# Where VectorE's program begins in its instruction memory: place 8 in place of place 72 behind a boundary of 128

## The chip, the cores and the metric

The kernel runs on one core of one Trainium2 chip. The metric is the time of one execution on the device, in microseconds (us). Three executions of the kernel before took 162.50, 162.59 and 162.71 us; their median is 162.59 us.

## What is computed

The reference rotates pairs of numbers (a rotary embedding) in a tensor of 16 x 512 x 1024 numbers of 32 bits, seen as 16 heads of 64 numbers each:

```python
x = x.reshape(batch, seq, num_heads, head_dim)        # 16, 512, 16, 64
x1, x2 = x[..., :32], x[..., 32:]
cos, sin = cos[None, :, None, :], sin[None, :, None, :]   # 512 x 32, shared by batch and head
rotated = np.concatenate([x1 * cos - x2 * sin, x1 * sin + x2 * cos], axis=-1)
```

So 33.6 MB come in, 33.6 MB go out, and each output needs two products and a sum. The two tables are 64 KB each.

## The kernel before

The input is cut into eight tiles of 4 MB (`NT = 8`): 128 partitions, each with eight rows of 1024 numbers. There are five buffers for a whole tile (`bufs`, name `x_sb`), and the result overwrites the input in place. Tile 0 is loaded in pieces of 1, 1, 2 and 4 rows, tile 1 in two pieces, the others whole. Tiles 5 to 7 go into the buffers of tiles 0 to 2, so their loads wait for the stores of these.

All loads of x and all stores are issued by SyncE's queue (SP) in one fixed order: loads 0 to 4, stores 0 to 2, loads 5 to 7, stores 3 to 7 (L178 to L188; the last store in three pieces, rows 0 to 2, 6 to 7, then 3 to 5). The two tables are loaded from ScalarE's queue (L90, L91). Every one of these transfers is cut into equal parts, one per DMA engine, of which there are 16, and it is complete when all 16 have ended their part. So each of the 16 moves the same number of bytes of x over the whole run.

The tables are spread to 128 partitions by four small matmuls (L113), and ScalarE writes the signed sine table (L118, L119). Each tile is then computed in groups of two or three rows, in an order written out by hand (`PLAN`): T multiplies the rows, halves swapped, by the signed sine table on GpSimd (L146; B is the same on VectorE), P multiplies them by the cosine on VectorE (L149), S adds the two on VectorE (L151). For some groups A does the product in place on VectorE (L153) and M adds with TensorE and ScalarE instead (L158 to L161).

Before all of that, L69 places VectorE's program. `addr_align(128, offset, max_nops=0)` asks the loader to put the next instruction of VectorE's stream `offset` places behind a multiple of 128 instruction places. The places in between are padding; with `max_nops=0` VectorE does not execute the padding but jumps over it. Nothing else of the program depends on that number.

In the trace VectorE has 82 instructions. Two belong to the opening barrier, then comes the jump of L69 (at 0.76 us, 47 ns). Behind it stand 79: the 48 tensor operations, 27 waits on semaphores that are instructions of their own, and four of the closing barrier. With the first of them in place 72, the 57th is in place 128: it is the wait ahead of the sum (L151) that starts at 112.10 us. The last is in place 150.

Of the kernel before, what the change touches and what calls it, by code (L numbers as in the profile page):

```python
# [12 lines left out]
def kernel(  # L13
# [8 lines left out]
    nc = tc.nc  # L22
# [43 lines left out]

    SYNC = mybir.DependencyInfo(mybir.DependencyClass.Sync, mybir.DependencyReason.DATA)

    nc.vector.addr_align(128, 72, max_nops=0)  # L69

    def implied(inst, *others):
        for o in others:
# [151 lines left out]
```

## Time and profile before

| what | value |
|---|---|
| median of three executions | 162.59 us |
| the profiled execution's own time | 162.54 us |
| its span, first to last instruction | 160.8 us |
| VectorE (DVE) busy | 138.4 us, 86% |
| GpSimd (POOL) busy | 130.2 us, 81% |
| TensorE (PE) busy | 61.1 us, 38% |
| ScalarE (ACT) busy | 14.1 us, 9% |
| DMA: bytes moved, mean rate | 67.25 MB, 418 GB/s |

The profile is of one execution. Its span is 1.74 us shorter than its own time; the rest lies ahead of the first and behind the last instruction. In the profile L149 is line 149 of the kernel. DVE is VectorE, POOL is GpSimd, SP is SyncE, and SPq or DVEq is the queue of that engine (waits, barriers and the issue of transfers). A DMA queue's row gives its packets, its megabytes and the time that these took as a share of all 16 DMA engines over the stretch asked for. The queue of kind "instruction" is the one that brings pieces of program.

### The profile page before, as it was taken

To read this page: it belongs to the slowest core of one execution; us is meant where nothing else is said; L and a number is where in the kernel's file an instruction comes from. 1 tells how busy PE (TensorE), PEld (TensorE's weight loads), DVE (VectorE), ACT (ScalarE), POOL (GpSimd) and SP (SyncE) were. 2 spreads that over 40 slices of the span, in tenths; PEclk is the share of its full clock that TensorE was granted. 3 is DMA by queue.
4 is the path that set the end of the run, shared out by engine and by line. 5 is a ranking of instruction groups with operands and counts; after the bars stand their busy time and mean duration, and the time that the engine had idled before them with its cause. 6 is when DMAs were issued, how large, how long until landed. Compare 5 with 4: busy or idle time off the path is not lost.

```text
span 160.8 us, 395 instructions
## 1 busy us (share of the span) xinstructions
PE 61.1 (38%) x84; PEld 18.8 (12%) x84; DVE 138.4 (86%) x48; ACT 14.1 (9%) x25; POOL 130.2 (81%) x29
## 2 busy tenths in 40 slices
PE   0500000140488803088881368877686800000000
PEld 0200000100122100032221022222222200000000
DVE  0069999999999999999999999999999999999200
ACT  3110000000011110011110011111212110000000
POOL 2299999999979299995999299999999999991000
PEclk9999999999999995555558555599999985555555
DMA  5999999999999999999999999999999999999994
GB/s 157 388 438 421 452 461 457 391 432 465 408 400 465 440 391 465 448 391 465 448 391 457 457 391 440 457 410 424 440 432 424 432 448 416 432 457 400 407 432 205
DMA packets 3329, 67.25 MB, mean 418 GB/s; under 512 B 384, under 2 KB 512, under 8 KB 768
## 3 DMA queue, kind: packets, MB, share of 16 engines
q1 hardware_dynamic: 3168, 67.11, 97.8%
q10 hardware_dynamic: 160, 0.13, 0.3%
q14 instruction: 1, 0.01, 0.0%
HBM read 33.69 MB, written 33.55 MB: 418 GB/s over the span
## 4 chain that ended last, share of the span: by engine, by line
DVE 81%; issue 5%; POOL 3%; DMA 3%; PE 1%; ACT 0%; DVEq 0%
DVE x_sb L151 38%; DVE pp L149 36%; DVE x_sb L153 6%; POOL T L146 3%; DMA tabs<-in_sin_dram 3%; DVE T L146 1%; PE pp L113 1%; ACT sns L118 0%; DVEq L151 0%; ACT sns L119 0%; DVEq L149 0%
## 5 line engine op out<-in xcount | busy, mean ns | idle before, releaser
L146 POOL TENSOR_TENSOR T<-x_sb,sns 128x3072 f32<-128x3072 f32 (+1 forms) x22 | 129.2, 5914 | 14.4 <-ACT sns L119 5.4
L149 DVE TENSOR_TENSOR pp<-x_sb,tab 128x3072 f32<-128x3072 f32 (+1 forms) x20 | 60.8, 3040 | 9.3 <-ACT tab L119 8.8
L151 DVE TENSOR_TENSOR x_sb<-T,pp 128x3072 f32<-128x3072 f32 (+1 forms) x20 | 60.7, 3033 | 2.0 <-POOL T L146 0.5
L158 PE MATMUL ps<-T,ident 128*128 128x512 f32 x40 | 31.8, 886 | 42.6 <-POOL T L146 27.2
L160 PE MATMUL ps<-x_sb,ident 128*128 128x512 f32 x40 | 29.9, 839 | 18.9 <-DVE x_sb L153 18.9
L161 ACT COPY x_sb<-ps 128x512 f32<-128x512 f32 x20 | 11.7, 586 | 108.7 <-PE ps L160 108.7
L158 PEld LDWEIGHTS ps<-T,ident 128*128 128x128 f32 x40 | 7.8, 245 | 66.4 <-ACT x_sb L161 29.2
L160 PEld LDWEIGHTS ps<-x_sb,ident 128*128 128x128 f32 x40 | 9.9, 259 | 36.0 <-DVE x_sb L153 24.4
L153 DVE TENSOR_TENSOR x_sb<-x_sb,tab 128x2048 f32<-128x2048 f32 x5 | 11.4, 2280 | 0.0
L146 DVE TENSOR_TENSOR T<-x_sb,tab 128x2048 f32<-128x2048 f32 x3 | 6.8, 2281 | 0.0
L113 PE MATMUL pp<-tabs,sel 64*128 64x256 f32 x2 | 1.2, 694 | 5.1 <-DMA tabs<-in_sin_dram 5.1
L113 PE MATMUL tab<-tabs,sel 64*128 64x256 f32 x2 | 1.2, 710 | 0.8 <-DMA tabs<-in_cos_dram 0.8
L118 ACT ACT_TABLE_LOAD x1 | 1.3, 1283 | 1.9 <-issue 1.9
L113 PEld LDWEIGHTS pp<-tabs,sel 64*128 64x128 f32 x2 | 0.5, 310 | 5.1 <-issue 5.1
L113 PEld LDWEIGHTS tab<-tabs,sel 64*128 64x128 f32 x2 | 0.5, 306 | 1.5 <-DMA tabs<-in_cos_dram 1.5
L118 ACT COPY sns<-pp 128x256 f32<-128x256 f32 x1 | 0.4, 373 | 3.1 <-PE pp L113 3.1
L98 POOL MEMSET ident<- 128x128 f32 x1 | 0.2, 204 | 0.3 <-POOLq L205 0.3
L119 ACT ACTIVATE sns<-pp 128x256 f32<-128x256 f32 x1 | 0.4, 389 | 0.0
L99 POOL TENSOR_SCALAR_AFFINE_SELECT ident<-ident 128x128 f32<-128x128 f32 x1 | 0.3, 292 | 0.1
L105 POOL COPY sel<-ident 64x128 f32<-64x128 f32 x1 | 0.3, 282 | 0.1
L118 ACT COPY tab<-pp 128x64 f32<-128x64 f32 x1 | 0.2, 197 | 1.4 <-PE tab L113 1.4
L205 POOL MEMSET const-float32-0.0<- 128x1 f32 x1 | 0.1, 99 | 0.2 <-issue 0.2
(4 smaller groups left out, 0.5 us busy)
## 6 DMA issues: line engine op xcount, KB each, us to landing
out_dram<-x_sb SPq DMA_DIRECT2D x7, 4096.0 KB, 22.0
x_sb<-in_x_dram SPq DMA_DIRECT2D x6, 4096.0 KB, 29.2
out_dram<-x_sb SPq DMA_DIRECT2D x2, 1536.0 KB, 13.0
x_sb<-in_x_dram SPq DMA_DIRECT2D x1, 2560.0 KB, 20.4
x_sb<-in_x_dram SPq DMA_DIRECT2D x1, 2048.0 KB, 11.8
x_sb<-in_x_dram SPq DMA_DIRECT2D x1, 1536.0 KB, 14.9
x_sb<-in_x_dram SPq DMA_DIRECT2D x2, 512.0 KB, 4.6
x_sb<-in_x_dram SPq DMA_DIRECT2D x1, 1024.0 KB, 7.4
```

Source lines behind the costliest of these rows:

```text
L99: nc.gpsimd.affine_select(out=ident, in_=ident, compare_op=ALU.not_equal, fill=1.0, base=0, pattern=[[-1, P]], channel_multiplier=1,)
L105: nc.gpsimd.tensor_copy(out=sel.rearrange("k (b p) -> k b p", b=BP), in_=bass.AP(tensor=i64.tensor, offset=i64.offset, ap=[i64.ap[0], [0, ...
L113: spread = [nc.tensor.matmul(out=o.rearrange("p r j -> p (r j)"), lhsT=sel, rhs=tabs[:, i], start=True, stop=True) for i, o in ((1, sin_ps ...
L118: signed.append(nc.scalar.copy(out=o[:, :, 1, :], in_=sin_ps[:, r0:r0 + o.shape[1], :]))
L119: signed.append(nc.scalar.mul(out=o[:, :, 0, :], in_=sin_ps[:, r0:r0 + o.shape[1], :], mul=-1.0))
L146: return [eng.tensor_tensor(out=Ts[t, k], in0=swapped(xr, n), in1=tb, op=ALU.mult)]
L149: return [nc.vector.tensor_tensor(out=pps[t, k], in0=xr, in1=cosb(k), op=ALU.mult)]
L151: return [nc.vector.tensor_tensor(out=xr, in0=Ts[t, k], in1=pps[t, k], op=ALU.add)]
L153: return [nc.vector.tensor_tensor(out=xr, in0=xr, in1=cosb(k), op=ALU.mult)]
L158: made.append(nc.tensor.matmul(out=ps, lhsT=ident, rhs=Ts[t, k][:, c * C:(c + 1) * C], start=True, stop=False))
L160: made.append(nc.tensor.matmul(out=ps, lhsT=ident, rhs=xc, start=False, stop=True))
L161: made.append(nc.scalar.copy(out=xc, in_=ps))
```

## The change

One number: the place of VectorE's first instruction behind the jump, counted from a multiple of 128 places, becomes 8. The 79 instructions stand in places 8 to 86 in place of 72 to 150. Which instructions run, on which engine, in which order and with which waits stays the same.

```diff
--- before
+++ after
@@ -66,7 +66,7 @@
 
     SYNC = mybir.DependencyInfo(mybir.DependencyClass.Sync, mybir.DependencyReason.DATA)
 
-    nc.vector.addr_align(128, 72, max_nops=0)
+    nc.vector.addr_align(128, 8, max_nops=0)
 
     def implied(inst, *others):
         for o in others:
```

## The prediction

> **What bounds the kernel now.** I read the page's DMA rows first, then the chain, then single stretches of the span. From the page:
>
> ```profile
> span 160.8 us, 395 instructions
> q1 hardware_dynamic: 3168, 67.11, 97.8%
> q14 instruction: 1, 0.01, 0.0%
> DVE x_sb L151 38%; DVE pp L149 36%; DVE x_sb L153 6%; POOL T L146 3%; DMA tabs<-in_sin_dram 3%; DVE T L146 1%; PE pp L113 1%; ACT sns L118 0%; DVEq L151 0%; ACT sns L119 0%; DVEq L149 0%
> ```
>
> The loads and stores of x (queue q1) fill 97.8% of what 16 DMA engines have over the span. The chain names VectorE, since its operations follow each other closely, but VectorE has time to spare: its last sum ends at 149.67 us and the store of it is issued at 149.70, while in the trace the store piece issued before it lands only at 156.28. The last piece would find the DMA engines taken for 6 us more. Earlier stores show the same, by their issue against the landing of the transfer ahead of them: store 1 56.80 against 62.53, store 2 66.14 against 72.20. Issue to first packet is 1.0 us at the start (0.73 to 1.73), so VectorE could be some 4 us late anywhere and the DMA engines would not run dry. The end is set by the DMA engine that ends its equal share last.
>
> Now the one packet of kind "instruction". In the stretch 107.6 to 108.1 us the DMA view has
>
> ```profile
> q1 hardware_dynamic: 11, 0.36, 175.2%
> q14 instruction: 1, 0.01, 4.0%
> ```
>
> and 4.0% of 16 engines for 0.5 us is 0.32 us. The packet's record: 8192 bytes, from 107.694 to 108.018, 324 ns. With the 128 places of the diff that is 64 bytes for an instruction: one block of 128. It is the only such packet in the span. The engine that carried it lost more than 324 ns: its next packet of x, 32 KB, took 1875 ns, where nearly all others of 32 KB took 1213 to 1221. The loss is 0.32 + 0.66, less some ns of overlap: 0.97 us.
>
> That loss is never made good. The landings of one transfer on its 16 engines show it: of the last load whose landing is ahead of the packet (tile 6), the last engine lands 0.06 us behind the last but one (101.31, 101.37); of the next (tile 7) it is 0.47 (111.09, 111.56), and 0.50, 0.50, 0.49, 0.49, 0.45, 0.42 and 0.42 for all that follow, to the last store (159.50, 159.92). The end of the run by stretches (columns: PE, PEld, DVE, ACT and POOL busy, PE clock, DMA share, GB/s):
>
> ```profile
> 158.00:158.50 0.50, 0.00 (x0) 0.00 (x0) 0.00 (x0) 0.00 (x0) 0.00 (x0) 0.50 0.98 418
> 158.50:159.10 0.60, 0.00 (x0) 0.00 (x0) 0.00 (x0) 0.00 (x0) 0.00 (x0) 0.50 0.40 164
> 159.10:159.60 0.50, 0.00 (x0) 0.00 (x0) 0.00 (x0) 0.00 (x0) 0.00 (x0) 0.50 0.06 25
> ```
>
> A share of 0.06 is one engine of 16: it alone works while the other 15 have ended. So the bound is one DMA engine, and 0.42 us of the end hang on that engine being late.
>
> **The change, part by part.** It moves the 79 instructions behind the jump from places 72 to 150 into places 8 to 86. Nothing is added on any queue.
>
> The crossing of place 128 goes. Is the packet at 107.694 VectorE's? The 57th instruction behind the jump is in place 128. The 56th is a product:
>
> ```profile
> 106.45 2.28 DVE L153 TENSOR_TENSOR x_sb<-x_sb,tab 128x2048 f32<-128x2048 f32 x1
> 108.64 3.35 DVE L149 TENSOR_TENSOR pp<-x_sb,tab 128x3072 f32<-128x3072 f32 x1
> 112.10 3.35 DVE L151 TENSOR_TENSOR x_sb<-T,pp 128x3072 f32<-128x3072 f32 x1
> ```
>
> It waits for the sum that ended at 106.53, so VectorE's sequencer reaches place 128 from then on; the packet starts 1.16 us later. The first load starts its first packet 1.00 us after its issue. That fits. VectorE itself loses nothing: the three rows follow one another without a gap beyond the usual wait. What the crossing costs is the DMA engine's 0.97 us, 0.42 of it at the end. With places up to 86 no boundary is crossed inside the kernel: minus 0.42 us.
>
> The jump. It is there before, too (47 ns at 0.76 us), so it costs nothing new by itself. New is where it lands. No packet of kind "instruction" lies between it and 107.69, so place 72 was in a block already there; place 8 may lie in the next block, 64 places from where the old jump landed. Then entering that block may bring a packet of 8192 bytes, as entering at place 128 did. Its time would be 0.80 + 1.16 = 1.96 us (estimate from the rows above). Two costs. First, VectorE: were it to wait for the packet, it would go on by about 1.96 + 0.97 = 2.9 us; its first wait to be met is that for the first piece of x, over at 4.70, and its first product starts at 8.83. Nothing, then, and 4 us more are covered by the stores' slack. Second, the DMA engine: at 1.96 us the first loads are just starting (first packets of the 16 engines at 1.73 to 2.3, some of them 4 KB in up to 1009 ns against a usual 159). Bounds: the loss there is between nothing (it lies in time in which the engine waits for its first data) and 0.97. It does not heal by itself later: the pattern of the first load's landings, nine engines, a gap of 0.23, seven engines, is still there at 101 us. But a loss shows at the end only by what exceeds the engine's lead: at 107.69 the late engine gave up 0.97 and ended 0.42 behind the last of the others, so it had been 0.55 ahead of it. A loss up to 0.55 is free; 0.97 costs 0.42 again. I take a loss below 0.55, since 0.32 is the packet's own time and the remaining 0.66 came from an engine with a full stream of 32 KB packets behind it. So 0 for the jump, with ends of 0 and +0.42 for this engine.
>
> The sum: 162.54 - 0.42 = 162.12 us for an execution like the profiled one; the median stands 0.05 above that execution, so 162.17, in round numbers 162.2.
>
> [...]
>
> **The rivals.**
> 1. The packet moves to the start and costs as much there. For it: the fixed shares and lags that don't heal. Against: DMA engines that are not streaming yet at 1.96. If the whole 0.97 is lost by the same engine, the end stays: 162.59; with part of it, between 162.17 and 162.59.
> 2. The packet isn't VectorE's. ScalarE sends off a copy at 106.68 and TensorE has handed out 110 instructions by 106.6, so either might cross a boundary there. Against it stands the count, which puts place 128 exactly there without a free number. No change then: 162.59. [...]
> 3. Slower: the packet at the start hits a DMA engine that is already among the last. Of the first load's landings (3.80 to 4.68), seven of 16 lie in the last 0.23 us. Its loss of 0.97 would stand at the end in full, in place of 0.42: +0.55, 163.14. It decides, with a loss of 0.97, from a lead below 0.97 - 0.42 - 0.33 = 0.22 us. Against it: if the same DMA engine carries it, its lead was 0.55. Two packets in a row on that engine (a block and the one behind it) would give 2 x 0.97 - 0.55 - 0.42 = +0.97, 163.56.
> 4. The jump does not leave the block it comes from, and no packet is left in the span: 162.17, as forecast, by another way.
>
> **How the numbers follow.** A measurement tells about 0.2% (0.33 us) from no change, so 162.27 and 162.92 are the borders. Mid-run packet gone and the start free or nearly so (with rival 4): 0.50, range 162.0 to 162.27. Rival 1: 0.24, spread from 162.27 to 162.7. Rival 2: 0.10. Rival 3 and its double: 0.16. So faster 0.50, same 0.34, slower 0.16. The range reaches from 162.0, where the DMA engine that is now the second to last ends 0.15 earlier, to 162.95, leaving out most of rival 3.
>
> **What would show it.** Right: no packet of kind "instruction" near 107.7; one near 2 us or none; the last engine's landing within 0.1 us of the last but one at the end; VectorE's first product at 8.8 and its last sum at 149.7, or both shifted together by less than 1 us. Rival 1 shows as a last landing 0.4 behind from the first loads on, rival 3 as 0.75 or more, rival 2 as the packet still at 107.7. The prediction is wrong if the lag comes back from the start, or if something outside the span grows: time minus span is 1.74 us now, and VectorE's instructions behind the kernel, which follow place 86, might now cross place 128.

## The result and the profile after

The kernel with place 8 takes 163.32 us (median of 22 executions, 162.74 to 165.07); the kernel before takes 162.66 us beside it (22 executions, 162.50 to 163.08). The ratio is 1.0047, with a 95% interval of 1.0028 to 1.0065: 0.5% slower where 0.2% faster was forecast. The spread is news as well: 2.3 us from the fastest to the slowest, 0.6 before.

The profiled execution after took 162.84 us, near the short end of that spread. From its page (span; a DMA queue's packets, megabytes and share of 16 engines; the chain by line):

```profile
span 161.1 us, 395 instructions
q1 hardware_dynamic: 3168, 67.11, 97.6%
q14 instruction: 1, 0.01, 0.0%
DVE x_sb L151 38%; DVE pp L149 36%; DVE x_sb L153 5%; DMA tabs<-in_sin_dram 3%; POOL T L146 3%; DVE T L146 1%; PE pp L113 1%; ACT sns L118 0%; ACT sns L119 0%; DVEq L151 0%; DVEq L149 0%
```

There is still one packet of program. It has left 107.7 us and lies in the stretch 2.9 to 3.4 us, as the DMA view of that stretch shows:

```profile
q1 hardware_dynamic: 47, 0.19, 98.3%
q14 instruction: 1, 0.01, 3.9%
```

Its record: 8192 bytes from 3.098 to 3.407 us. The 98.3% beside it are to be noted: the DMA engines are already fully at work. The end of the span by stretches (last two columns: DMA share and GB/s):

```profile
158.00:158.50 0.50, 0.00 (x0) 0.00 (x0) 0.00 (x0) 0.00 (x0) 0.00 (x0) 0.50 0.98 418
158.50:159.10 0.60, 0.00 (x0) 0.00 (x0) 0.00 (x0) 0.00 (x0) 0.00 (x0) 0.50 0.25 102
159.10:159.60 0.50, 0.00 (x0) 0.00 (x0) 0.00 (x0) 0.00 (x0) 0.00 (x0) 0.50 0.06 25
159.60:160.00 0.40, 0.00 (x0) 0.00 (x0) 0.00 (x0) 0.00 (x0) 0.00 (x0) 0.50 0.00 0
```

A share is booked to the stretch in which a packet starts. From 158.5 to 159.1 the share is 0.25 where it was 0.40 before: the DMA engine in the middle of the 16 lands earlier (the median landing is at 159.09 us, 159.32 before), but the last two land later, at 159.71 and 160.23 (159.50 and 159.92 before). The last one sets the end. VectorE starts its first product 0.14 us later and its last sum 0.53 us later. No DMA engine waits for it: the last store is issued at 150.24 us, and the piece ahead of it lands only at 156.58. VectorE's first and last operation:

```profile
8.97 2.30 DVE L149 TENSOR_TENSOR pp<-x_sb,tab 128x2048 f32<-128x2048 f32 x1 [8.97 <-ACT tab L119]
...
146.85 3.35 DVE L151 TENSOR_TENSOR x_sb<-T,pp 128x3072 f32<-128x3072 f32 x1
```

### The profile page after: what moved, and what is told of

Same layout as the page of the kernel before. It is cut to its first block, busy times and chain, and to the rows that moved or that the text cites. A ratio compares the mean times of both kernels' runs of the same rounds, so it can differ in the third digit from the quotient of the medians.

```text
span 161.1 us, 395 instructions
## 1 busy us (share of the span) xinstructions
PE 57.1 (35%) x84; PEld 17.7 (11%) x84; DVE 138.4 (86%) x48; ACT 14.1 (9%) x25; POOL 130.2 (81%) x29
## 3 DMA queue, kind: packets, MB, share of 16 engines
q1 hardware_dynamic: 3168, 67.11, 97.6%
## 4 chain that ended last, share of the span: by engine, by line
DVE 81%; issue 5%; DMA 3%; POOL 3%; PE 1%; ACT 0%; DVEq 0%
DVE x_sb L151 38%; DVE pp L149 36%; DVE x_sb L153 5%; DMA tabs<-in_sin_dram 3%; POOL T L146 3%; DVE T L146 1%; PE pp L113 1%; ACT sns L118 0%; ACT sns L119 0%; DVEq L151 0%; DVEq L149 0%
## 5 line engine op out<-in xcount | busy, mean ns | idle before, releaser
L158 PE MATMUL ps<-T,ident 128*128 128x512 f32 x40 | 29.7, 834 | 47.0 <-POOL T L146 27.5
L160 PE MATMUL ps<-x_sb,ident 128*128 128x512 f32 x40 | 27.8, 784 | 19.0 <-DVE x_sb L153 19.0
L160 PEld LDWEIGHTS ps<-x_sb,ident 128*128 128x128 f32 x40 | 9.3, 244 | 34.9 <-DVE x_sb L153 24.4
L119 ACT ACTIVATE sns<-pp 128x256 f32<-128x256 f32 x1 | 0.4, 390 | 0.0
```

The source lines that it names most:

```text
L119: signed.append(nc.scalar.mul(out=o[:, :, 0, :], in_=sin_ps[:, r0:r0 + o.shape[1], :], mul=-1.0))
L158: made.append(nc.tensor.matmul(out=ps, lhsT=ident, rhs=Ts[t, k][:, c * C:(c + 1) * C], start=True, stop=False))
L160: made.append(nc.tensor.matmul(out=ps, lhsT=ident, rhs=xc, start=False, stop=True))
```

## The experiments

Two theories. **P**: the packet makes one DMA engine late, that engine's last landing is the end, and the time depends on when in the run the packet comes. **Q**: VectorE itself loses time by the jump, and the end with it. The times of the kernel before, beside each set, are 162.71, 162.65 and 162.83 us.

The trace gives, for every transfer, its 16 landings. The table has one profiled execution per row; the kernels are described below it. "Late" is the last landing less the median of the 16, in us, at four transfers: the piece of tile 0's load that is complete at about 9 us, the load of tile 3 (43), of tile 6 (101) and of tile 7 (111), and then the last store.

| run | packet at (us) | late at 9 | 43 | 101 | 111 | end | its time |
|---|---|---|---|---|---|---|---|
| before | 107.69 | 0.33 | 0.32 | 0.34 | 0.72 | 0.60 | 162.54 |
| before again | 107.86 | 0.24 | 0.29 | 0.35 | 0.90 | 0.89 | 162.71 |
| after | 3.10 | 0.81 | 0.81 | 0.93 | 1.05 | 1.14 | 162.84 |
| after again | 3.58 | 1.20 | 1.25 | 1.58 | 2.50 | 2.60 | 164.31 |
| place 48 | 3.16 | 0.77 | 0.78 | 0.77 | 0.86 | 0.98 | 162.74 |
| second jump, new block | 44.02 | 0.23 | 0.27 | 1.34 | 1.82 | 1.86 | 163.78 |
| no jump | 125.88 | 0.41 | 0.42 | 0.87 | 1.70 | 1.79 | 163.39 |
| less work, place 68 | none | 0.29 | 0.31 | 0.34 | 0.33 | 0.39 | 162.04 |
| less work, place 8 | 3.47 | 1.03 | 1.05 | 1.15 | 1.30 | 1.37 | 163.18 |
| less work, second jump | 44.54 | 0.15 | 0.15 | 0.69 | 1.04 | 1.13 | 162.93 |
| place 8, jump inside the block | 3.77 | 1.42 | 1.45 | 2.02 | 2.63 | 2.74 | 164.28 |
| place 8, jump to a new block | 3.68, 46.00 | 1.16 | 1.18 | 2.16 | 2.14 | 2.14 | 163.85 |
| less work, ScalarE jumps | 58.07 | 0.16 | 0.17 | 0.58 | 0.57 | 0.56 | 162.18 |
| less work, SyncE jumps | 115.99 | 0.28 | 0.26 | 0.77 | 1.11 | 1.61 | 163.18 |

In all 14, the execution's time is the last landing plus 2.60 to 2.66 us, and the median landing of the last store is the same within 0.4 us (158.94 to 159.32). What differs in time is how late the last DMA engine is. The packet is not the only thing that makes one late: with no jump and with SyncE's jump an engine falls behind near 52 and near 111 us, ahead of the packet.

**No jump at all.**

```diff
-    nc.vector.addr_align(128, 72, max_nops=0)
+    pass
```

> L69 left out: no jump, VectorE's program stands where the stream before it ends (place N). Theory P (one packet of 8192 bytes makes one DMA engine late, and the time follows when in the run that happens): a crossing of a boundary in the middle of a full stream, one packet of kind instruction somewhere behind 3 us, last landing 0.3 to 0.6 us behind the last but one at the end, time as before, 162.66 +- 0.2, narrow spread. Theory Q (VectorE's jump itself costs): 162.6, and also no jump. Theory R (place of VectorE's instructions matters in another way than by the packet): not to be told.

162.64 us (162.39 to 163.39, 10 executions), ratio 0.9996 (0.9981 to 1.0012): no difference in the median, as P and Q both had it, but not the narrow spread that was expected. The packet is at 125.88 us, 1.2 us after VectorE could hand over its 63rd instruction behind the opening barrier (the product at 124.67). If the packet marks place 128 here as it did before, the 64th instruction is in place 128, and the program, left alone, begins in place 65. That fits with a jump to place 72 that brings no packet, and with places 48 and 8 in the next block. The profiled execution is the longest of the ten, and not by the packet: the late engine is late before it (0.42 to 0.85 around the first change from loads to stores, near 52 us, then 1.70 at 111). The packet makes a second engine late (0.79 behind the median from 131 us on, where the last but one was 0.21 behind), and the end does not change by that.

**Place 48**, where no boundary is crossed inside the kernel either.

```diff
-    nc.vector.addr_align(128, 72, max_nops=0)
+    nc.vector.addr_align(128, 48, max_nops=0)
```

> Places 48 to 126, no crossing inside the kernel. If the jump stays in its block (N below 48): no packet in the span; theory P: the last two landings at the end within 0.1 us, 162.2. If it goes to the next block: a packet near 3 us as with place 8; P: 163.3 with a wide spread (162.7 to 165). Theory Q: 163.3 when the jump is long, without regard to a packet.

163.30 us (162.74 to 164.08), ratio 1.0035 (1.0017 to 1.0053), a packet at 3.16 us: the same loss as with place 8, within the intervals. It is not the number 8 that matters; what the two have in common is the packet at the start.

**The changed kernel once more**, for a second profile.

> The changed kernel once more, for a second profiled execution. Theory P: packet near 3 us, the last landing 0.5 us or more behind the last but one from the first loads on, and the end later than 159.50 (the end without the late engine before) by just that lag. Theory Q: VectorE's first product later than 9 us and its last sum later than 150.5, with the stores waiting for it and DMA engines idle.

163.19 us (162.76 to 164.31), ratio 1.0037 (1.0015 to 1.0058). The profiled execution took 164.31 us. The end of its span by stretches:

```profile
158.50:159.10 0.60, 0.00 (x0) 0.00 (x0) 0.00 (x0) 0.00 (x0) 0.00 (x0) 0.50 0.20 82
159.10:159.60 0.50, 0.00 (x0) 0.00 (x0) 0.00 (x0) 0.00 (x0) 0.00 (x0) 0.50 0.06 25
159.60:160.10 0.50, 0.00 (x0) 0.00 (x0) 0.00 (x0) 0.00 (x0) 0.00 (x0) 0.50 0.06 25
160.10:160.60 0.50, 0.00 (x0) 0.00 (x0) 0.00 (x0) 0.00 (x0) 0.00 (x0) 0.50 0.06 25
160.60:161.10 0.50, 0.00 (x0) 0.00 (x0) 0.00 (x0) 0.00 (x0) 0.00 (x0) 0.50 0.06 25
```

For 2 us one DMA engine works alone (0.06 of 16). It was 1.20 late at 9 us and 2.50 at 111. Against the first profiled execution of the same kernel the time is 1.47 us longer and the last landing 1.48 us later, so in these two the spread is that of the lateness. P's sum for the end, 159.50 plus the distance of the last landing from the last but one (1.83), gives 161.33; it came at 161.71, since the last but one was late as well (159.87). VectorE is late as Q had it (first product at 9.84, last sum ended at 150.70), but the store piece ahead of its last store lands only at 158.08, so no DMA engine waits for it.

**The packet in the middle**: place 72, and a second jump ahead of tile 2.

```diff
     for t in range(NB):
+        if t == 2:
+            nc.vector.addr_align(128, 40, max_nops=0)
         compute(t)
```

> Place 72 at L69 as before, and a second jump ahead of tile 2 (at some 42 us) to place 40 of the next block: one packet, at some 43 to 45 us in place of 107.7, in a full stream. Theory P with the start as the reason: as before, 162.66 +- 0.2, narrow, lag at the end 0.4 to 0.6. A variant of P in which the lag grows with the time that it lasts: 162.8 to 163.1. Theory Q: VectorE stands still for 1 us or more at the second jump and the time rises to 163.3.

162.91 us (162.68 to 163.78), ratio 1.0016 (0.9998 to 1.0035): between the two kernels, and not clearly apart from either (place 48, in the same set: 1.0017 to 1.0053). The variant of P with a growing lag had expected 162.8 to 163.1. The profiled execution is the longest of the ten; its late engine takes 0.98 at the packet (0.27 at 43 us, 1.25 at 53) and 0.48 more between 101 and 111 us. VectorE does not stand still for the packet: the second jump starts at 40.41 us, the next instruction runs at 40.94, and the packet comes at 44.02. So the packet does not bring the instruction that VectorE jumped to; what it does bring no run shows.

**The packet alone, VectorE taken out.** Tiles 5 to 7 are loaded and stored but not computed (their output is their input). VectorE's program ends early and, from place 68, crosses no boundary.

```diff
-    nc.vector.addr_align(128, 72, max_nops=0)
+    nc.vector.addr_align(128, 68, max_nops=0)
...
     for t in range(NB, NT):
-        compute(t)
         store(t, *((0, 3), (6, 8), (3, 6)) if t == NT - 1 else ())
```

> Tiles 5 to 7 are loaded and stored but not computed, so that VectorE's program (places 68 to 121) crosses no boundary while the stores run. Theory P (the end is the landing of the one DMA engine that the packet made late): no packet of kind instruction in the span; last landing at the end within 0.2 us of the last but one unless something else makes an engine late; time 162.1 to 162.3, below the kernel before by 0.4. Theory Q (VectorE's or the jump's own time): the same as the next two kernels, since VectorE has nothing to do in the last 60 us.

The same with place 8 in place of 68:

> As the kernel with places from 68, tiles 5 to 7 not computed, with place 8 at L69. Theory P: one packet near 3 us, lag 0.6 to 1.1 us from the load of tile 0's last piece on, time 0.8 to 1.1 us over the one from place 68, so 163.0 to 163.3, although VectorE's last sum is 50 us ahead of the end. Theory Q: no difference between the two, since VectorE's delay has no work behind it that is late.

And with place 68 and the second jump of the experiment above:

> As the kernel with places from 68, tiles 5 to 7 not computed, with a second jump ahead of tile 2 (to place 40 of the next block): one packet near 44 us. Theory P with an early packet costing more: between the other two, 162.6 to 162.9. P with the same cost wherever the packet lies: as the kernel with place 8. Theory Q: no difference.

162.26 us (162.04 to 162.59), 163.76 (162.91 to 164.34) and 163.35 (162.93 to 164.46); ratios to the kernel before 0.9969 (0.9955 to 0.9982), 1.0056 (1.0035 to 1.0078) and 1.0045 (1.0024 to 1.0067). The first has no row of kind "instruction" on its page, and its end by stretches is

```profile
158.00:158.50 0.50, 0.00 (x0) 0.00 (x0) 0.00 (x0) 0.00 (x0) 0.00 (x0) 0.50 1.09 467
158.50:159.10 0.60, 0.00 (x0) 0.00 (x0) 0.00 (x0) 0.00 (x0) 0.00 (x0) 0.50 0.06 21
159.10:159.60 0.50, 0.00 (x0) 0.00 (x0) 0.00 (x0) 0.00 (x0) 0.00 (x0) 0.50 0.00 0
```

with nothing started after 159.1: no engine stands apart (last landing 159.41, last but one 159.31). With place 8, VectorE's last operation and the end are

```profile
97.19 3.35 DVE L151 TENSOR_TENSOR x_sb<-T,pp 128x3072 f32<-128x3072 f32 x1
```

```profile
158.50:159.10 0.60, 0.00 (x0) 0.00 (x0) 0.00 (x0) 0.00 (x0) 0.00 (x0) 0.50 0.25 102
159.10:159.60 0.50, 0.00 (x0) 0.00 (x0) 0.00 (x0) 0.00 (x0) 0.00 (x0) 0.50 0.06 25
159.60:160.30 0.70, 0.00 (x0) 0.00 (x0) 0.00 (x0) 0.00 (x0) 0.00 (x0) 0.50 0.04 18
```

VectorE has ended 60 us ahead, and the kernel is still 1.50 us slower than with place 68. Q falls, and a packet of VectorE costs. That one at 3 us costs more than one at 44 us is not shown here: the two ratio intervals overlap for the most part. The losses of 1.50 and 1.09 us are higher than the 0.8 to 1.1 and the 0.3 to 0.6 expected; why stays open. Against the kernel before they are 1.11 and 0.70 us, where the full kernels with the same jumps have 0.66 and 0.20, but there too the intervals overlap.

**Two jumps.** Place 8 and a second jump ahead of tile 2, first to place 40, then to place 8.

```diff
-    nc.vector.addr_align(128, 72, max_nops=0)
+    nc.vector.addr_align(128, 8, max_nops=0)
...
+        if t == 2:
+            nc.vector.addr_align(128, 40, max_nops=0)
```

> All tiles computed; place 8 at L69 and a second jump ahead of tile 2 to place 40 of the next block: two packets, near 3 and near 44 us. Theory P with both on the same DMA engine: the lag of the last engine grows by about 1 us at 44 us, time 164.2 (0.9 over place 8 alone). P with two different DMA engines: one more late engine, the last one unchanged, 163.3. Theory Q: VectorE's products start no later than with place 8, 163.3.

One packet only, at 3.77 us: the edit missed what it was for. VectorE is in place 31 there, so place 40 lies in the block that it is in. It is of use as a control: a jump inside the block brings no packet and costs nothing that the times show, 163.30 us (162.67 to 164.28) against 163.32 with place 8 alone. In its profiled execution the late engine loses 0.48 between 43 and 54 us all the same, with no second packet. With the second jump to place 8:

```diff
-            nc.vector.addr_align(128, 40, max_nops=0)
+            nc.vector.addr_align(128, 8, max_nops=0)
```

> All tiles computed; place 8 at L69 and a second jump ahead of tile 2 to place 8 of the next block, which place 31 behind the first jump can't reach inside its block: two packets, near 3 and near 44 us. If both come over the same DMA engine: lag 0.6 to 1.1 at 43 us, 1.6 to 2.1 at 54, time 164.2 to 164.6. If over different ones: lag unchanged at 54 us, two late engines, 163.3.

164.35 us (163.85 to 164.74, 4 executions), ratio 1.0091 (1.0067 to 1.0114), and on the page

```profile
q14 instruction: 2, 0.02, 0.0%
```

The distance of the last landing from the last but one goes from 0.84 (43 us) to 1.75 (54 us). The second packet takes 0.33 us and the packet of x behind it 1875 ns in place of 1213, which accounts for that. No second engine stands apart (the last but one is 0.38 behind the median), so both packets came over the same DMA engine, and their losses add up, as P had it for that case. In time the kernel with two packets is 1.52 us above the kernel before beside it, where place 8 alone is 0.66 above its own: 0.86 us for the second, from four executions.

**Another engine's packet, and a late one.** VectorE as in the kernel with place 68 (no packet of its own); ScalarE jumps ahead of tile 2:

```diff
+        if t == 2:
+            nc.scalar.addr_align(128, 8, max_nops=0)
         compute(t)
```

> Tiles 5 to 7 not computed and VectorE from place 68 (no packet of its own in the span: 162.26 so far). ScalarE jumps ahead of tile 2, at some 55 us, to place 8 of its next block. Theory P, for any engine's program: one packet at 56 to 60 us, one DMA engine 0.5 to 1.0 late from then on, 162.8 to 163.3. If the cost were VectorE's own: 162.3.

or SyncE jumps inside the last store:

```diff
-        store(t, *((0, 3), (6, 8), (3, 6)) if t == NT - 1 else ())
+        if t < NT - 1:
+            store(t)
+    store(NT - 1, (0, 3))
+    nc.sync.addr_align(128, 8, max_nops=0)
+    store(NT - 1, (6, 8), (3, 6))
```

> Tiles 5 to 7 not computed and VectorE from place 68. SyncE jumps between the first two pieces of the last store, issued at some 111.4 us, to place 8 of its next block: one packet at 112 to 116 us, behind the last change from loads to stores (110 us). P with the direct loss alone (0.97 less the lead): 162.7 to 163.1, narrow. P in which a late engine loses again at the changes between loads and stores: lower than the packet near 44 us (163.35) and the one near 3 us (163.76) for that reason. If the cost were VectorE's own: 162.3.

162.44 us (162.18 to 162.78) and 162.79 (162.48 to 163.18). The kernel without a packet (162.26) ran in another set, so the ratios to the kernel before have to be compared: 0.9979 (0.9968 to 0.9989) with ScalarE's jump and 0.9995 (0.9985 to 1.0005) with SyncE's, against 0.9969 (0.9955 to 0.9982) without a packet. ScalarE's packet, in the stretch 58.0 to 58.5 us, is

```profile
q1 hardware_dynamic: 13, 0.43, 200.0%
q14 instruction: 1, 0.01, 3.9%
```

and from then on one engine is 0.3 to 0.4 us behind the last but one, where it was 0.01 before. So a packet of another engine's program also makes one DMA engine late. In time ScalarE's packet costs nothing that can be told from no packet; P had expected 0.5 to 1.0 and missed. SyncE's late packet costs 0.35 us by the medians, each taken against the kernel before beside it; that is less than in both less-work kernels with an earlier packet of VectorE (1.09 and 1.50), as P had it, and 162.79 lies in the 162.7 to 163.1 expected. But ScalarE's packet at 58 us costs less still, so the time at which the packet comes is not all that decides. In SyncE's profiled execution three DMA engines were already late from 50 and 110 us on, so its row tells little of the packet.

**The kernel before again.**

> The kernel before, for a second profiled execution. Theory P: one packet near 107.7 us; the last landing at the end 0.4 to 1.0 us behind the last but one, by the lead that the hit DMA engine happened to have, and the execution's time 2.6 us over its last landing. Theory Q has no expectation.

162.98 us (162.58 to 163.20), ratio to the runs of the same kernel beside it 1.0007 (0.9997 to 1.0017). The packet is at 107.86, the next one of x takes 1875 ns again, and the last landing is 0.53 behind the last but one.

## Why the prediction was wrong

- **The bound** (one DMA engine that ends its share last) was right: 14 executions from 162.04 to 164.31 us, all 2.60 to 2.66 us behind their last landing.
- **The packet is VectorE's**: right. It followed the place of VectorE's program from 107.7 to 3.1, 44, 46 and 125.9 us, which ends rival 2. **Removing it gives 0.42**: this fits. Without any packet the time is 162.26 against 162.65, 0.39 less, but in a kernel with less VectorE work; no full kernel without a packet was run.
- **The jump costs nothing**: this step failed, in its second half. That a packet may come at the start was said. The price put on it, "I take a loss below 0.55" and "So 0 for the jump", was wrong three times over. First, the time: not 1.96 us but 3.10 to 3.77, when the DMA engines already stream (98.3%). Second, the loss: in the execution after, the packet takes 0.31, the next two packets of x on that engine 367 and 487 ns in place of 159, together 0.31 + 0.21 + 0.33 = 0.85 us, nearly the 0.97 of the middle. The other five executions with a packet at the start have the same three (309 to 369, 313 to 379 and 487 ns), and the sum is 0.84 to 0.86 in all six. Third, the lead: 0.55 of it was counted as free, from one execution at 107.7 us. At 9 us the late engine is 0.58 to 1.09 behind the last but one in these six, against 0.42 at the end before. With 0.85 lost, that leaves a lead between 0.27 and none at all.
- **"It does not heal"** was right, but not all. A late engine often loses again: between 101 and 111 us, where loads give way to stores, its distance from the median grew by 0.92, 0.61, 0.48, 0.35, 0.15, 0.12, 0.09 and -0.02 in the eight executions with a packet before 50 us (0.83 in the one without a jump), by -0.01 with ScalarE's packet at 58, by 0.34 ahead of SyncE's packet, and by -0.01 in the one that had no late engine. In the nine in which it grew, some 32 KB packets that start between 108.5 and 110.5 us take 1.30 to 2.24 us in place of 1.21; in the three in which it did not, none does. An early packet leaves its engine late ahead of more such places than one at 107.7. That lateness is the reason for the second loss was not shown: ahead of SyncE's packet engines fell behind near 52 us (0.26 to 0.65) that had not been late.
- **The sum**: with -0.39 for the packet that goes, the measured +0.66 leaves some +1.05 for the one that comes, where the prediction had 0. That is worked back from the result and is no test of its own. The packet's own 0.85 is seen in the traces; what the leads take off it and the second losses add was not told apart.
- **The rivals**: rival 3 (the packet at the start hits an engine that is already among the last, and costs more than it did in the middle, 163.14) came nearest, with a chance of 0.16, and 0.18 us too cheap. Its sign, a last landing 0.75 or more behind from the first loads on, shows at 9 us in four of the six executions; the other two (0.58 and 0.61) lie between it and rival 1's 0.4. The range ended at 162.95, just where it left this case out. Rival 1 (equal cost) had the loss nearly right (0.97 for 0.85) and, like the forecast, too large a lead.
- **VectorE is covered**: right; half a microsecond late (its last sum starts 0.53 us later), and with 60 us to spare (less work, place 8) the end was late all the same. The part outside the span is 162.84 - 161.1 = 1.74 us, as before, so nothing came from behind the kernel.
- **What VectorE waits and what the kernel pays**: VectorE shows no more than the usual gap at the crossing before (0.09 us ahead of the sum at 112.10, as ahead of the next one at 121.03; 0.10 ahead of the same sum after, at 112.64, where no packet is near), and after the jump its first product, at 8.97 us, follows ScalarE's table (L119), 5.56 us behind the end of the packet. The kernel, whose end is set by a DMA engine, does pay: against the kernel without a packet (which computes less), and by medians, each taken against the kernel before beside it, VectorE's packet costs 0.4 us at 107.7, 1.0 at 3 us, and two cost 1.9.

## What to carry to other kernels

In this kernel all 16 DMA engines had equal shares and were taken for 97.8% of the span before and 97.6% after, and what one of them did besides was paid at the end, as far as that engine had no lead: of the 0.97 us that the packet at 107.7 took from one engine, 0.42 stood at the end. A packet of program at 3 us cost 0.66 us more than one at 107.7; for times in between no order was shown. Look for such a loss in the landings of each transfer: a last one that stands apart from the other 15, from some moment to the end. Jumps to another block of program brought one here (to places 8 and 48 at L69 a packet at 3.10 to 3.77 us, to place 40 or 8 ahead of tile 2 one at 44.0 to 46.0); before costing it at nothing, ask what the DMA engines are doing when its packet arrives, and count no engine's lead that was read from one execution.

## What was not expected of the hardware

- The packet behind a jump of VectorE came 2.3 to 4.6 us after it (0.80 to 3.10; 41.43 to 46.00), behind those of ScalarE and SyncE 3.8 and 3.9 us, not the 1.16 us that the crossing suggested. VectorE did not wait for it: its next instruction ran 0.5 us after the jump in the three executions with a jump to a new block ahead of tile 2, and 0.2 us after the jump inside the block.
- Among 32 KB loads the packet of x behind it took 1875 ns in all five cases seen; among stores 1354, 1447 and 1667 ns, so the loss there was 0.45 to 0.76 us and not 0.97.
- No kernel that computes everything was found without the packet: from place 65 on, where the packet at 125.88 us puts the program without a jump, VectorE's 75 instructions ahead of the closing barrier reach place 139, and the jumps ahead of them that left the block (to places 8 and 48) brought a packet of their own.
